# The decay logits of a gated linear attention as one float32r product per half sequence

## Chip, cores and metric

The kernel runs on one core of a Trainium2 chip. The metric is the device time of one execution in microseconds. Before the change it was 1006.1 us (median of 3 runs, 1002.45 to 1006.14).

## What is computed

A decoder trunk of two layers over 1024 tokens of width 1024. Each layer projects the normalised input into three groups of heads (sliding-window attention, retention, gated linear attention), and projects their joined outputs back. The change concerns the decay of the gated linear attention (GLA): 16 low-rank channels `ga` of the input projection are multiplied by a 16x128 matrix, a bias is added, and the logarithm of a sigmoid of it is the decay per token and key channel.

```
proj = h @ w_in
(aq, ak, av, ag, rq, rk, rv, rg, gq, gk, gv, gg, ga) = jnp.split(proj, IN_SPLITS, axis=-1)
...
gate_logits = (ga @ gla_gate_w + gla_gate_b).astype(jnp.float32)
log_a = (jax.nn.log_sigmoid(gate_logits) / GLA_GATE_NORMALIZER).reshape(B, S, GLA_HEADS, GLA_DK)
g = gated_linear_attention(gq, gk, gv, log_a)
```

The tensors are float32. `GLA_GATE_RANK` is 16, and 4 heads of 32 key channels give 128 columns.

## The kernel before

**Tiling.** Tokens lie in 8 tiles of 128 (`t` = 0 to 7). The large products run on TensorE in the type float32r. A float32 operand is kept as two float32r parts, high (the rounded value) and low (the rest), and a product is the sum of three passes: high by high, low by high, high by low (`PASSES`). The arenas hold the parts of the input tiles (`hT`) and of the weights; a weight chunk is loaded into a staging tile `st` by a transfer from SyncE's queue, then split by ScalarE or VectorE (high part) and VectorE or GpSimd (low part).

**Before layer 0.** `mod_first` computes the modulation vectors from `c`; `pre` normalises a token tile: two squares with sums on ScalarE (L654), their sum and scale on VectorE (L643, L637), a power on GpSimd (L638), the scaling on VectorE (L669), eight transposes on TensorE (L178), the modulation (L701 on ScalarE, L703 on VectorE), and the split into high and low (L707, L711). The first two token tiles are prepared while `mod_first` runs, the third and fourth while TensorE works on the first gate products, the other four later.

**Gates.** A layer begins with the gate projections. `do_gates` projects two token tiles for `gg` (272 columns: 256 of the GLA gate and the 16 channels `ga`), then two for `rg` (the retention gate), and so on in layer 0; layer 1 does six tiles of `gg` before `rg`. Each `gg` tile starts `gla_logits` (L993): ScalarE copies the 16 channels out of the PSUM bank (L995), `silu2` computes the gate (L987 on ScalarE, L989 on VectorE) and SyncE stores it to `sgS`. Later the 128x16 copy is transposed by TensorE into 16 rows (L1001), and ScalarE copies these into columns of `gaT` (L1002), whose row 16 and those behind it are ones from a fill (L784).

**Decay logits.** When four token tiles are in `gaT` (32 partitions by 512 tokens), `gla_log` multiplies it by `gwt` (L1011). `gwt` is a 32x128 float32 tile for each layer: 16 rows of the matrix, one row of the bias, and zeros. ScalarE and VectorE turn the result into the log decay (L1014 to L1019). There are two such products per layer, four in all. The tiles 4 to 7 are transposed only after the first product has read `gaT` (`("z", l, 0)`).

**Order.** TensorE runs in the order in which the program is written. That order is decided at build time by a planner: `clk` is a clock of estimated TensorE time, to which `mult` and `transp` add a cost; side work is put in generators (`job`), which go on as soon as `clk` has passed a due time; the table `L` holds these distances. `pump` is called after every 7 products. For a float32 product of 512 columns `mult` adds 4 x 512 / 2400 = 0.853, for a float32r product 512 / 2400 = 0.213. The other engines' orders, and that of SyncE's queue, are made by the framework's scheduler from the program and its dependences.

**Retention.** After the gates the retention runs: `ret_rot` (VectorE, L820 to L825 and L1151) turns the projections, `ret_core` transposes them, ScalarE copies the transposes (L147 by way of `copy("rT", ...)`), TensorE multiplies, VectorE masks (L1173) and updates the state (L1192, L1194). Beside it, VectorE accumulates the modulation rows of the gate and of the next layer from `w_mod` chunks (L365), each after its own transfer into a staging tile, and the weights of the coming stages are loaded and split (L147, L149, L535).

Of the kernel before, what the change touches and what calls it, by code (L numbers as in the profile page):

```python
# [10 lines left out]
F32 = mybir.dt.float32  # L11
F32R = mybir.dt.float32r
I32 = mybir.dt.int32
AF = mybir.ActivationFunctionType
ALU = mybir.AluOpType
AX = mybir.AxisListType

P = 128
# [3 lines left out]
NT = S // P  # L22
# [69 lines left out]
def trunk(ctx: ExitStack, tc: tile.TileContext, ins, cst, out):  # L92
    nc = tc.nc
    V, A, G, T = nc.vector, nc.scalar, nc.gpsimd, nc.tensor
    x_in, c_in, pos_in, w_mod, b_mod, pre_g, post_g, w_in, sinks, gw_in, gb_in, gn_in, w_out = [
        ins[n] for n in _INS
    ]

    cp = ctx.enter_context(tc.tile_pool(name="const", bufs=1))
    bp = ctx.enter_context(tc.tile_pool(name="big", bufs=1))  # L100
    gp = ctx.enter_context(tc.tile_pool(name="work", bufs=2))
# [5 lines left out]
    def nm(s):  # L107
        uid[0] += 1
        return f"{s}_{uid[0]}"
# [4 lines left out]
    def t1(dt=F32):  # L114
        return gp.tile([P, 256], dt, tag="t1", name=nm("t1"), bufs=B1)
# [4 lines left out]
    def small(w, dt=F32):  # L120
        return gp.tile([P, w], dt, tag="sm", name=nm("sm"), bufs=BS)
# [4 lines left out]
    def aux(dt=F32):  # L126
        return ps.tile([P, 512], dt, tag="aux", name=nm("aux"), bufs=8 - MMB)

    def f(ap):
        return ap.bitcast(F32)  # L130
# [20 lines left out]
    def dma(k, dst, src):  # L151
        {"S": nc.sync, "A": A, "P": G}[EN[k]].dma_start(dst, src)
# [24 lines left out]
    def transp(dst, src, idn):  # L177
        T.transpose(dst, src, idn)  # L178
        clk[0] += 0.056 if src.dtype == F32R else 0.109

    def lat(key, l):

        return L[key + "@1"] if l and key + "@1" in L else L[key]
# [4 lines left out]
    def flag(name, lat=0.0):  # L188
        flags[name] = clk[0] + lat
# [41 lines left out]
    def cload(name, dt=F32, eng=nc.sync):  # L231
        a = cst[name]
        t = cp.tile(list(a.shape), dt, name="c_" + name)
        eng.dma_start(t, a)
        return t
# [3 lines left out]
    ident = cload("ident", eng=A)  # L239
# [540 lines left out]
    gat = []  # L780

    def new_ga():
        gat.append(gp.tile([P, NT * P], F32, tag="kT1", name=nm("gaT"), bufs=1)[0:32, 0:512])
        G.memset(gat[-1], 1.0)  # L784
    stR = cp.tile([P, 2, P], F32, name="stR")
    stG = cp.tile([P, 4, 64], F32, name="stG")
    stC = cp.tile([P, 64], F32, name="stC")
# [16 lines left out]
    for l in range(DEPTH):  # L804
        V.tensor_copy(sink8[:, l].rearrange("p (m r) -> p m r", r=2),
                      sinkn[:, 8 * l:8 * l + 8].rearrange("p (r m) -> p m r", r=2))
    gwt = cp.tile([32, 2, P], F32, name="gwt")
    V.memset(gwt, 0.0)
    for l in range(DEPTH):
        nc.sync.dma_start(gwt[0:16, l, :], gw_in[l])  # L810
        nc.sync.dma_start(gwt[16:17, l, :], gb_in[l:l + 1, :])
    def rotary(dst, src, nh, t, kind):

        s4 = src.rearrange("p (h c k) -> p h c k", h=nh, c=2)
        sn = sincos[:, t, 0, kind * 32:kind * 32 + 32]
        cs = sincos[:, t, 1, kind * 32:kind * 32 + 32]
        b = gp.tile([P, 256], F32, tag="tr", name=nm("tr"), bufs=1)
        b4 = b[:, 0:nh * 64].rearrange("p (h c k) -> p h c k", h=nh, c=2)
        d4 = dst.rearrange("p (h c k) -> p h c k", h=nh, c=2)
        V.tensor_tensor(d4, s4, cs.unsqueeze(1).unsqueeze(1).to_broadcast((P, nh, 2, 32)), ALU.mult)  # L820
        snb = sn.unsqueeze(1).to_broadcast((P, nh, 32))
        V.tensor_tensor(b4[:, :, 0, :], s4[:, :, 1, :], snb, ALU.mult)
        V.tensor_tensor(b4[:, :, 1, :], s4[:, :, 0, :], snb, ALU.mult)
        V.tensor_tensor(d4[:, :, 0, :], d4[:, :, 0, :], b4[:, :, 0, :], ALU.subtract)
        V.tensor_tensor(d4[:, :, 1, :], d4[:, :, 1, :], b4[:, :, 1, :], ALU.add)  # L825
# [158 lines left out]
    def silu2(pg):  # L984

        th = t1()
        A.activation(th, pg, AF.Tanh, scale=0.5)  # L987
        sg = t1()
        V.scalar_tensor_tensor(sg, th, 1.0, pg, ALU.add, ALU.mult)  # L989
        return sg  # L990


    def gla_logits(l, t, pg, pa):  # L993
        ga = small(16)
        A.activation(ga, pa, AF.Copy)  # L995
        dma("ssg", sgS[t], silu2(pg))
        yield lat("gz1", l)
        if t >= 4:
            yield (0.0, ("z", l, 0))
        pt = aux()  # L1000
        transp(pt[0:16, 0:P], ga, ident)  # L1001
        A.activation(gat[l][0:16, (t % 4) * P:(t % 4 + 1) * P], pt[0:16, 0:P], AF.Copy)  # L1002
        flag(("ga", l, t), lat("gz2", l))

    las = {}
# [454 lines left out]
    def layer(l):  # L1460
        if l == 0:
            job(table_job())
        new_ga()
        def do_gates(name, p):
            w = used(l, name)
            for t in (2 * p, 2 * p + 1):
                pg = mm()
                if name == "gg":
                    project(pg[:, 0:272], l, t, w, 272)
                    job(gla_logits(l, t, pg[:, 0:256], pg[:, 256:272]))  # L1470
                else:
                    project(pg[:, 0:256], l, t, w)
                    dma("ssr", srS[t], silu2(pg[:, 0:256]))
                pump()
            if p == NP_ - 1:
                load(l, "rk" if name == "gg" else "rv")
            if name == "gg" and p % 2:
                job(gla_log(l, p // 2))
# [228 lines left out]
```

## Time and profile before

| | |
|---|---|
| median of 3 runs | 1006.1 us (1002.45 to 1006.14) |
| span of the profiled execution | 1008.9 us |
| TensorE busy (PE) | 975.4 us, 97% |
| weight loads (PEld) | 829.5 us, 82% |
| VectorE (DVE) | 684.5 us, 68% |
| ScalarE (ACT) | 408.8 us, 41% |
| GpSimd (POOL) | 234.4 us, 23% |

The span is from the first to the last instruction of the profiled execution; the page gives no other time for it.

How to read the lines that follow. A page line of an engine gives its busy time, the share of the span, and the number of instructions. The chain that ended last is followed back from the last instruction, at each step to what released it. A line of the windows gives a stretch in us from the span's start, its length, the busy time and number of instructions of TensorE, weight loads, VectorE, ScalarE and GpSimd, then the granted TensorE clock (1.00 is full speed), the share of the transfer engines and GB/s. A line of the timeline gives the start and the time taken in us, the engine, the line of the kernel, the operation, `output<-inputs` and the shape; "x4" are four instructions that follow each other, and in brackets stand the idle time before the first and what ended it. SPq and ACTq are the transfers issued by SyncE and ScalarE. A line of the grouped instructions ends with the busy time in us, the mean time of one in ns, and the idle time before them. A line of the chain in order of time gives start, time taken and what.

A matmul's record has a latency at its end that overlaps the next one, so the cost of a matmul in a row of them is the distance from start to start.

### The profile page before, as it was taken

Reading aid. Unit: us, or ns where it says so; the run is one execution under the profiler, and the core shown is the slowest. Engines: PE = TensorE matmul, PEld = TensorE weight load, DVE = VectorE, ACT = ScalarE, POOL = GpSimd, SP = SyncE. Lnnn points to the kernel's source line nnn. Section 1 sums busy time; section 2 is a strip of 40 time slices with the busy share of each in tenths; the row PEclk is TensorE's granted clock in tenths of the full one; section 3 lists DMA queues with packets and bytes.
Section 4 is the critical chain, followed back from the end, with each engine's and each line's share of the span. In section 5 each row is a group of like instructions: output and inputs, shape, how many; then the busy total and the mean of one; then the engine's idle time right before and its main releaser. Section 6 shows DMA issues by size and latency. Waiting matters only on the chain.

```text
span 1008.9 us, 19610 instructions
## 1 busy us (share of the span) xinstructions
PE 975.4 (97%) x7137; PEld 829.5 (82%) x7137; DVE 684.5 (68%) x1680; ACT 408.8 (41%) x1152; POOL 234.4 (23%) x275
## 2 busy tenths in 40 slices
PE   5899999899999999999999999999999999999897
PEld 1499999888998777778889999998899877777785
DVE  3789857757666778564578275785666577566876
ACT  2476311223322656632465232123332256663321
POOL 2310001223320234330112000113332034544100
PEclk8899999999999999999999999999999999999999
DMA  9942513623326355577655251353132434378883
GB/s 293 308 137 76 173 45 100 170 81 96 96 74 199 89 149 163 171 239 244 214 157 173 64 158 32 108 150 100 41 104 85 125 90 130 112 236 249 265 263 140
DMA packets 129836, 148.73 MB, mean 147 GB/s; under 512 B 14046, under 2 KB 94152, under 8 KB 129740
## 3 DMA queue, kind: packets, MB, share of 16 engines
q1 hardware_dynamic: 124044, 137.92, 45.3%
q10 hardware_dynamic: 5696, 9.56, 2.6%
q8 instruction: 56, 0.92, 0.4%
q14 instruction: 40, 0.33, 0.1%
HBM read 109.17 MB, written 36.18 MB: 144 GB/s over the span
## 4 chain that ended last, share of the span: by engine, by line
PE 80%; DVE 8%; DMA 7%; issue 2%; POOL 1%; ACT 1%; SPq 0%; POOLq 0%; DVEq 0%; ACTq 0%
PE mm L163 61%; PE aux L163 14%; PE aux L178 5%; DMA st<-in_w_in_dram 2%; DMA st<-in_w_out_dram 1%; POOL sm L638 1%; DMA xk<-in_x_dram 1%; DMA wm<-in_w_mod_dram 1%; DMA t<-aoS 1%; DVE arena L535 1%; DMA st<-in_w_mod_dram 1%; DMA t<-sgS 1%; DVE t L328 0%; DVE st L572 0%; DMA mixF<-t 0%
## 5 line engine op out<-in xcount | busy, mean ns | idle before, releaser
L163 PE MATMUL mm<-arena 128*128 128x256 f32 (+2 forms) x1824 | 299.2, 318 | 1.8 <-ACT arena L707 1.8
L163 PE MATMUL mm<-arena,arena 128*128 128x256 f32 (+2 forms) x1824 | 300.7, 318 | 0.0
L163 PEld LDWEIGHTS mm<-arena 128*128 128x128 f32 x1824 | 254.6, 191 | 26.5 <-issue 4.1
L163 PEld LDWEIGHTS mm<-arena,arena 128*128 128x128 f32 x1824 | 254.1, 189 | 25.5 <-issue 4.6
L638 POOL TENSOR_TENSOR sm<-sm,mhalf 128x1 f32<-128x1 f32 (+1 forms) x64 | 56.1, 877 | 347.0 <-DVE sm L637 328.6
L163 PE MATMUL mm<-arena,mx 128*128 128x512 f32 (+1 forms) x564 | 132.4, 392 | 2.9 <-ACT kept L1335 2.9
L163 PEld LDWEIGHTS mm<-arena,mx 128*128 128x128 f32 x564 | 103.1, 191 | 27.1 <-ACT kept L1335 3.3
L147 ACT ACTIVATE t<-aux 128x256 f32<-128x256 f32 (+2 forms) x124 | 55.7, 467 | 76.1 <-PE aux L178 64.8
L147 ACT ACTIVATE arena<-st 128x512 fp32r<-128x512 f32 x94 | 56.1, 626 | 59.1 <-DMA st<-in_w_in_dram 21.4
L535 POOL TENSOR_TENSOR arena<-st,arena 128x512 fp32r<-128x512 f32 x31 | 43.2, 1395 | 138.9 <-ACT arena L147 100.9
L926 POOL TENSOR_TENSOR smx<-smx,sm 128x512 f32<-128x512 f32 x32 | 36.1, 1127 | 124.3 <-DVE sm L925 116.1
L535 DVE TENSOR_TENSOR arena<-st,arena 128x512 fp32r<-128x512 f32 x77 | 59.5, 795 | 6.1 <-ACT arena L147 4.1
L922 ACT ACTIVATE smx<-smx,sm 128x129 f32<-128x129 f32 x128 | 49.9, 392 | 28.4 <-DVE sm L919 28.4
L178 PE MATMUL aux<-c_ident,t 128*128 128x128 f32 (+1 forms) x292 | 48.8, 285 | 7.6 <-DVE t L669 7.2
L365 DVE SCALAR_TENSOR_TENSOR acc<-st,c_act,acc 128x512 f32<-128x512 f32 x60 | 45.5, 759 | 12.6 <-DMA st<-in_w_mod_dram 12.1
L178 PEld LDWEIGHTS aux<-c_ident,t 128*128 128x128 f32 (+1 forms) x292 | 35.4, 145 | 15.2 <-DVE t L669 9.0
L701 ACT ACTIVATE t<-aux,mod,mod 128x128 f32<-128x128 f32 x68 | 25.9, 458 | 43.8 <-DVE t L1242 18.2
L970 ACT ACTIVATE t<-aux 128x256 f32<-128x256 f32 x32 | 12.3, 383 | 75.5 <-PE aux L163 63.4
L163 PEld LDWEIGHTS aux<-t,mx 32*128 32x128 f32 (+1 forms) x896 | 39.5, 187 | 3.8 <-issue 2.1
L163 PE MATMUL aux<-t,mx 32*128 32x32 f32 (+1 forms) x896 | 40.7, 273 | 0.0
L917 DVE COPY_PREDICATED smx<-c_curmask,aux 128x256 f32<-128x256 int32 x64 | 25.5, 447 | 18.8 <-ACT smx L147 15.3
L1242 DVE SCALAR_TENSOR_TENSOR t<-t,sm,t 128x512 f32<-128x512 f32 x32 | 24.0, 779 | 18.6 <-DMA t<-in_x_dram 11.9
(220 smaller groups left out, 1384.3 us busy)
## 6 DMA issues: line engine op xcount, KB each, us to landing
st<-in_w_in_dram SPq DMA_DIRECT2D x96, 256.0 KB, 3.1
st<-in_w_mod_dram SPq DMA_DIRECT2D x64, 256.0 KB, 3.3
st<-in_w_out_dram SPq DMA_DIRECT2D x52, 256.0 KB, 3.8
mx<-mixS SPq DMA_DIRECT2D x20, 512.0 KB, 6.2
mixS<-t SPq DMA_DIRECT2D x72, 128.0 KB, 2.3
wm<-in_w_mod_dram SPq DMA_DIRECT2D x12, 512.0 KB, 8.0
t<-in_x_dram SPq DMA_DIRECT2D x24, 256.0 KB, 4.8
t<-tabS SPq DMA_DIRECT2D x16, 256.0 KB, 3.7
```

What stands on the lines that cost most here:

```text
L147: A.activation(dst, src, AF.Copy)
L163: T.matmul(dst, lhsT, rhs, start=start, stop=stop)
L178: T.transpose(dst, src, idn)
L365: V.scalar_tensor_tensor(acc, wt, c_act[:, k:k + 1], acc, ALU.mult, ALU.add)
L535: e.tensor_tensor(lo, st, f(hi), ALU.subtract)
L638: G.tensor_tensor(r, r, mhalf[:, :w], ALU.pow)
L701: A.activation(hf[:, ks], at[kt], AF.Identity, scale=gain, bias=shift)
L917: V.copy_predicated(sv, curmask.unsqueeze(1).to_broadcast((P, 2, P)), pv[:, :, n // P - 1, :])
L922: A.activation(sm[:, h, :], sm[:, h, :], AF.Exp, bias=mx[:, h:h + 1], accum_out=sums[:, h:h + 1])
L926: eng("pn").tensor_tensor(sm[:, :, 0:128], sm[:, :, 0:128], rs.unsqueeze(2).to_broadcast((P, 4, P)), ALU.mult)
L970: A.activation(sq, po, AF.Square)
L1242: V.scalar_tensor_tensor(xt[j], yg[j], r, xt[j], ALU.mult, ALU.add)
```

## The change

The product's operands become float32r with 128 contracted rows. `ga` is now a tile of its own (tag `ga`, 6 buffers) with three groups of 16 columns: high, low, high. ScalarE writes the two high groups with one copy (32 columns), and VectorE subtracts the high part from the PSUM value for the low group. The transpose makes 48 rows of it. `gwt` is built from a float32 tile `gwf` (from the `t1` buffers): rows 0 to 15, 16 to 31 and 32 to 47 hold the matrix, rows 48 and 49 the bias, the rest zeros. A copy rounds all of it to float32r, and a subtraction replaces rows 32 to 48 by the low parts. Contracting high, low, high with high, high, low gives the three passes of the split product in one matmul; the rows of ones meet the two bias rows, and zeros from row 50 on.

```diff
     def new_ga():
-        gat.append(gp.tile([P, NT * P], F32, tag="kT1", name=nm("gaT"), bufs=1)[0:32, 0:512])
-        G.memset(gat[-1], 1.0)
+        gat.append(gp.tile([P, NT * P], F32R, tag="kT1", name=nm("gaT"), bufs=1)[:, 0:512])
+        G.memset(f(gat[-1]), 1.0)
...
-    gwt = cp.tile([32, 2, P], F32, name="gwt")
-    V.memset(gwt, 0.0)
+    gwt = cp.tile([P, 2, P], F32R, name="gwt")
+    gwf = t1()
+    V.memset(gwf, 0.0)
     for l in range(DEPTH):
-        nc.sync.dma_start(gwt[0:16, l, :], gw_in[l])
-        nc.sync.dma_start(gwt[16:17, l, :], gb_in[l:l + 1, :])
+        c = slice(P * l, P * l + P)
+        for r in (0, 16, 32):
+            nc.sync.dma_start(gwf[r:r + 16, c], gw_in[l])
+        nc.sync.dma_start(gwf[48:50, c], gb_in[l:l + 1, :].to_broadcast((2, P)))
+    gwv = gwf.rearrange("p (l n) -> p l n", l=2)
+    V.tensor_copy(gwt, gwv)
+    V.tensor_tensor(gwt[32:49], gwv[32:49], f(gwt[32:49]), ALU.subtract)
...
     def gla_logits(l, t, pg, pa):
-        ga = small(16)
-        A.activation(ga, pa, AF.Copy)
+        ga = gp.tile([P, 3, 16], F32R, tag="ga", name=nm("ga"), bufs=6)
+        A.activation(ga[:, 0:3:2], pa.unsqueeze(1).to_broadcast((P, 2, 16)), AF.Copy)
+        V.tensor_tensor(ga[:, 1], pa, f(ga[:, 0]), ALU.subtract)
         dma("ssg", sgS[t], silu2(pg))
         yield lat("gz1", l)
         if t >= 4:
             yield (0.0, ("z", l, 0))
         pt = aux()
-        transp(pt[0:16, 0:P], ga, ident)
-        A.activation(gat[l][0:16, (t % 4) * P:(t % 4 + 1) * P], pt[0:16, 0:P], AF.Copy)
+        transp(pt[0:48, 0:P], f(ga).rearrange("p a n -> p (a n)"), ident)
+        A.activation(gat[l][0:48, (t % 4) * P:(t % 4 + 1) * P], pt[0:48, 0:P], AF.Copy)
```

The product itself (`mult(z, gwt[:, l, :], gat[l], True, True)`) is written as before. The table `L` of the planner is not changed.

## The prediction

> **What bounds the kernel now.** I read the page first: which engine is full, and which work the chain that ended last runs through.
>
> ```profile
> PE 975.4 (97%) x7137; PEld 829.5 (82%) x7137; DVE 684.5 (68%) x1680; ACT 408.8 (41%) x1152; POOL 234.4 (23%) x275
> ...
> PE 80%; DVE 8%; DMA 7%; issue 2%; POOL 1%; ACT 1%; SPq 0%; POOLq 0%; DVEq 0%; ACTq 0%
> ```
>
> TensorE (PE) is busy 97% and carries 80% of that chain. A share is an average, so next come the stretches in which the four changed products lie, with TensorE's busy time in each.
>
> ```profile
> 50.70:196.50 145.80, 145.26 (x1196) 139.83 (x1194) 112.83 (x313) 61.68 (x147) 18.19 (x17) 1.00 0.39 111
> ...
> 431.00:605.00 174.00, 173.96 (x1103) 152.88 (x1103) 108.37 (x249) 72.59 (x200) 27.32 (x32) 1.00 0.58 180
> 605.00:690.00 85.00, 82.32 (x666) 77.35 (x665) 56.66 (x168) 21.18 (x45) 12.85 (x12) 1.00 0.34 102
> ```
>
> In the first two TensorE stands still for 0.54 and 0.04 us. Time taken off it there moves everything behind it forward, as far as the next stall. Those stalls are the third thing I read, with the granted clock (the 1.00, 0.50 after the engines' columns).
>
> ```profile
> 47.10:49.60 2.50, 1.01 (x10) 0.77 (x8) 2.06 (x5) 0.00 (x0) 1.83 (x2) 1.00 0.56 146
> ...
> 199.62 1.23 PE L163 MATMUL aux<-t 64*128 64x128 f32 x8 [3.09 <-ACT t L147]
> ...
> 205.00:206.00 1.00, 1.00 (x8) 1.00 (x7) 0.00 (x0) 0.00 (x0) 0.00 (x0) 0.65 0.01 1
> ...
> 680.77 0.72 PE L163 MATMUL aux<-t 64*128 64x128 f32 x8 [1.28 <-ACT t L147]
> ...
> 946.33 3.92 PE L163 MATMUL mm<-arena,mx 128*128 128x512 f32 x9 [2.89 <-ACT kept L1335]
> ...
> 946.40:948.00 1.60, 1.60 (x4) 1.31 (x5) 1.60 (x4) 0.05 (x1) 0.00 (x0) 0.50 0.67 187
> 948.00:950.00 2.00, 2.00 (x6) 1.54 (x6) 1.38 (x4) 0.68 (x2) 0.26 (x1) 0.55 0.77 206
> ```
>
> A stall has a second price here. After 2.89 and 3.09 us of standing still TensorE got half its clock: in the one case from 946.3 until about 949.8 (a mean of 0.55 over 2 us is 1.8 us at 0.50), so 3.5 us at half rate, 1.7 us lost; in the other from 199.6 until about 205.7, 6.1 us, 3.0 us lost. After the 1.5 us stall ahead of 49.63 the clock stayed at 1.00.
>
> **What is removed: four float32 products.** Each is recorded as two passes.
>
> ```profile
> 577.84 1.12 PE L163 MATMUL aux<-gaT,gwt 32*128 32x512 f32 x2
> 578.89 0.39 PE L178 MATMUL aux<-c_ident,sm 128*16 128x128 f32 x2
> ...
> 687.37 4.81 PE L163 MATMUL mm<-arena 128*128 128x512 f32 x20
> 692.02 0.38 PE L178 MATMUL aux<-c_ident,t 128*128 128x128 f32 x2
> ```
>
> From the start of the product to the start of what follows is 578.89 - 577.84 = 1.05 us. The new product has float32r operands, 128 contracted rows and 512 columns, as the arena products of the second pair: (692.02 - 687.37) / 20 = 0.23 us. One product saves 0.82 us, four 3.3 us. If nothing but one pass were spared, the bound from below would be half of 1.05, or 2.1 us for all four; from above it is 3.3 us. I take 3.3, since the arena rows have the same type and shape.
>
> **What is added on TensorE: nothing that counts.** The 16 transposes still stream 128 identity columns; only the stationary side grows from 16 to 48 columns.
>
> ```profile
> L178 PE MATMUL aux<-c_ident,t 128*128 128x128 f32 x288 | 48.0, 285 | 7.6 <-DVE t L669 7.2 <-DVE mx L1115 0.3
> ...
> L178 PE MATMUL aux<-c_ident,sm 128*16 128x128 f32 x16 | 4.2, 272 | 0.0
> ```
>
> Between 16 and 128 stationary columns lie 13 ns: at most 16 x 13 = 0.2 us, at least nothing. I take nothing.
>
> **What is added on the other engines.** VectorE (DVE) gets 16 subtractions of 128x16 out of PSUM; the nearest row is the 128x16 copy.
>
> ```profile
> 12.81 0.25 DVE L277 COPY sm<-aux 128x16 f32<-128x16 f32 x2
> ...
> 125.00:150.00 25.00, 25.00 (x218) 24.46 (x217) 14.31 (x51) 3.99 (x9) 2.18 (x2) 1.00 0.18 57
> ```
>
> That is 0.13 us each, 2.0 us in all, half of it per layer, plus some 0.8 us for filling, rounding and subtracting the weight tile (256 columns each). In layer 0 TensorE runs without a pause past 125, and in the 25 us after it VectorE is idle for 10.7 us, so a backlog of 2 us is worked off there. If that cover were gone, its price is those 2 us per layer at most. The ScalarE copies into `ga` write 32 columns in place of 16; the 48-row copy out of PSUM is as long per partition as the 16-row one (some ns each). The larger fill of `gaT` has the same 512 columns per partition. All at nothing.
>
> SyncE gets four more small transfers, in front of the gate stores of layer 0.
>
> ```profile
> 52.07 0.43 SPq L810 DMA_DIRECT2D gwt<-in_gla_gate_w_dram  x1
> ...
> 53.29 0.28 SPq L811 DMA_DIRECT2D gwt<-in_gla_gate_b_dram  x1
> 54.94 1.38 SPq L152 DMA_DIRECT2D sgS<-t  x2
> 56.44 0.38 SPq L152 DMA_DIRECT2D st<-in_w_in_dram  x1
> ...
> 59.40 0.88 DVE L669 TENSOR_SCALAR t<-t,sm 128x512 f32<-128x512 f32 x2
> ...
> 106.26 0.41 DVE L820 TENSOR_TENSOR t<-mm,sincos 128x256 f32<-128x256 f32 x1
> ```
>
> Eight at about 0.38 us end near 55.1, where the first store was issued at 54.94: 0.2 us on a store that nothing reads for 100 us. VectorE's rounding of the weights waits for them, but stands in its order behind the scaling of the fifth token tile (59.40 before), after the last should have landed. The weight load issued at 56.44 and those behind it now stand behind two more stores; the first product with these weights is read at 106.26, so even 10 us would be hidden. Nothing.
>
> **What moves.** The orders of TensorE are nearly the same: 0.64 us less on the planner's clock shifts a few transposes by 7 to 10 products. One move on ScalarE (ACT) does count. In the changed program the first copy into `ga` stands between the squares of the third and of the fourth token tile; before, it stood behind all of them, at 53.95.
>
> ```profile
> 43.87 0.61 ACT L654 ACTIVATE t<-mx 128x512 f32<-128x512 f32 x1
> ...
> 45.00 0.19 ACT L654 ACTIVATION_READ_ACCUMULATOR t<-mx 128x1 f32 x1
> 50.33 1.50 ACT L701 ACTIVATE t<-aux,mod,mod 128x128 f32<-128x128 f32 x4 [5.14 <-PE aux L178]
> ...
> 53.95 0.18 ACT L995 ACTIVATE sm<-mm 128x16 f32<-128x16 f32 x1
> ...
> 46.76 0.15 DVE L643 TENSOR_TENSOR sm<-sm 128x1 f32<-128x1 f32 x1
> ...
> 48.09 1.88 DVE L669 TENSOR_SCALAR t<-mx,sm 128x512 f32<-128x512 f32 x2 [0.44 <-POOL sm L638]
> ...
> 45.83 1.41 PE L163 MATMUL mm<-arena 128*128 128x272 f32 x10
> 47.08 1.04 PE L178 MATMUL aux<-c_ident,t 128*128 128x128 f32 x8
> 49.63 1.09 PE L178 MATMUL aux<-c_ident,t 128*128 128x128 f32 x8 [1.52 <-DVE t L669]
> ...
> 52.68 5.92 PE L163 MATMUL mm<-arena,arena 128*128 128x256 f32 x48
> ```
>
> The copy needs the first gate product, whose last matmul is the third of the ten that start at 45.83: it starts at 46.1 and ends near 46.4. ScalarE now waits for that, and the fourth tile's two squares (1.2 us, done at 45.2 before) end near 47.85. Behind them hang VectorE's sum (46.76 before, now 47.9), GpSimd's power, the scaling, and the transposes for which TensorE already stood 1.52 us. Each comes 1.1 us later, so that stall becomes 2.6 us: a loss of 1.1 us. Bounds: 0 if the product ends early enough, and 1.1 plus a clock drop of 1.7 to 3.0 us if 2.6 us is already too long. The rows leave 1.5 to 2.9 us open; 2.6 lies nearer the upper end, but no row shows a drop below 2.89, so I keep the clock in the sum and the drop as a rival.
>
> [...]
>
> The delay should go no further. The second copy into `ga` now stands ahead of the third tile's modulation (50.33 before) and waits for the second gate product, which ends where the 48 arena products begin; modulation, rounding and subtraction (1.5 + 1.2 + 1.3 us) then fit into the 5.9 us of these 48 before TensorE reads that tile, and the fourth follows a projection later.
>
> **Sum.** -3.3 + 1.1 = -2.2 us. The page gives its span of 1008.9 us and no other time for that execution; the other runs took 1002.45 to 1006.14, median 1006.1, so the span is 2.8 above it. Changes of 2 us carry over: 1006.1 - 2.2, rounded to 1004.
>
> **Rivals.**
>
> *The gain is swallowed by the stalls behind it.*
>
> ```profile
> 192.30 5.80 DMA st<-in_w_in_dram
> ```
>
> The stall at 199.62 ends with this weight transfer (the ScalarE copy that TensorE waits for stands behind a conversion that needs it); the 1.28 us at 680.77 are the same wait in layer 1. If such loads land by the clock and not by TensorE's progress, an earlier arrival only waits longer, and 1.1 us of loss at the start is swallowed too, or remains: 1006 to 1007. Against it: those loads wait for buffers that VectorE frees in step with TensorE's products.
>
> *The clock drops in the longer stall at 48 us.* -3.3 + 1.1 + 1.7 to 3.0 = -0.5 to +0.8: 1005.5 to 1007.
>
> *The stall at 199.62 gets shorter than what lowers the clock.* Orders in the retention stretch ahead of it shift by several products, so the ScalarE copy that is late there may come before the weight transfer. Cut from 3.09 to 1.5 us and without 3.0 us of half rate: -2.2 - 4.6 = -6.8, or -8.3 without any stall: 998 to 999.
>
> *Slower: VectorE stands in order behind a mod-weight transfer while TensorE needs it.*
>
> ```profile
> 165.96 5.29 DMA st<-in_w_mod_dram
> ...
> 171.34 0.75 DVE L365 SCALAR_TENSOR_TENSOR acc<-st,c_act,acc 128x512 f32<-128x512 f32 x1 [3.83 <-DMA st<-in_w_mod_dram]
> ...
> 172.48 0.71 PE L163 MATMUL aux<-t 64*128 64x128 f32 x6 [0.54 <-DVE t L963]
> ```
>
> For 3.83 us VectorE waited, and TensorE felt 0.54 of it. In the changed program these accumulations sit elsewhere among the retention work. If TensorE feels nearly the whole transfer (5.3 us), the stall grows by 3.3 to 4.8 us and, from about 2.9 us on, the clock drops for 3.0 more: -2.2 + 6.3 to 7.8 = +4.1 to +5.6, 1010 to 1012. Against it: the planner's distances there are several microseconds, and only one such stall exists now.
>
> *The change does not do what it says*: the type could leave the product at two passes of 1.05 us. Then only the 1.1 us remains, 1007; the arena rows speak against it.
>
> **How the numbers follow.** Forecast 0.40, swallowed 0.13, clock drop 0.12, shorter stall 0.17, VectorE in order 0.15, no faster product 0.03. About 0.5% (5 us) is what a measurement of this kernel can tell from no change. The forecast, swallowed gain, clock drop and unchanged product lie within it. Faster by more: the shorter stall, plus 0.03 for forecast cases that save a part of it: 0.20. Slower by more: VectorE in order, plus 0.05 of the swallowed and clock cases if they fall together: 0.20. Same 0.60. The range runs from the shorter stall, 998.5, to the lower part of the slow case, 1011.
>
> **What would show it.** Right: four single records of the product near 0.4 us each with 0.23 us to the next start; the copy into `ga` at about 46.4 and a stall near 2.6 us ahead of the fourth tile's transposes, with the clock at 1.00 behind it; the stalls near 197, 680 and 945 about 2 us earlier and as long as before. Wrong: two records per product; a clock of 0.5 at 51; a new TensorE stall above 2 us between 105 and 195; a stall near 197 that is gone.

## The result, and the profile after

The changed kernel is slower: a median of 1009.8 us (20 runs, 1006.9 to 1016.23) against 1005.43 us (20 runs, 1000.95 to 1009.52) before on the same chip, a ratio of 1.0047 with a 95% interval of 1.0033 to 1.0062. That is 4.7 us more (3.3 to 6.2), where 2.1 us less were forecast (1004.0 against 1006.1).

The profiled execution of the changed kernel is one of its faster ones (1008.22 us for a span of 1006.5). That of before has a span of 1008.9 us. With the same 1.7 us between span and time it took about 1010.6 us, an estimate, and that is longer than each of the 20 runs. The two spans therefore stand the wrong way round, and only stretches can be compared in them.

First the engines' line of the changed kernel's page.

```profile
PE 970.6 (96%) x7133; PEld 828.4 (82%) x7133; DVE 688.9 (68%) x1698; ACT 411.3 (41%) x1152; POOL 233.5 (23%) x275
```

TensorE does 4 matmuls fewer (7133 for 7137) and is busy 4.8 us less in these two executions; VectorE has 18 instructions more (16 subtractions of the channels, two for the weight tile). The product does what it says, as the timeline of the changed kernel shows (start, time taken, then what; in brackets the idle time before it and what ended it):

```profile
84.94 4.58 PE L163 MATMUL mm<-arena 128*128 128x256 f32 x24 [2.01 <-DVE t L995]
89.84 1.12 PE L163 MATMUL mm<-arena,arena 128*128 128x272 f32 x7 [0.32 <-DVE t L995]
90.80 0.40 PE L163 MATMUL aux<-gaT,gwt 128*128 128x512 f32 x1
91.04 1.91 PE L163 MATMUL mm<-arena,arena 128*128 128x272 f32 x14
...
100.12 3.14 PE L163 MATMUL mm<-arena 128*128 128x256 f32 x24 [0.73 <-DVE t L995]
```

One record of 0.40 us, and 91.04 - 90.80 = 0.24 us to the next start; before it was 1.05. But there are three stalls that the kernel before doesn't have: 2.01, 0.32 and 0.73 us, 3.06 us together, in which a gate product waits for L995. In the changed kernel that is the VectorE multiplication that ends `silu2` (L989 before): it is the last reader of a gate product's PSUM bank, and the `mm` bank is free only behind it. Before, TensorE went through the same place without a pause:

```profile
80.07 6.00 PE L163 MATMUL mm<-arena 128*128 128x256 f32 x48
85.90 1.04 PE L163 MATMUL mm<-arena,arena 128*128 128x272 f32 x7
```

The next view shows why the banks come free late: the instructions of the tanh in `silu2`, what its engine idled for before it, and who waited for it. First the changed kernel, where it is L993.

```profile
L993 ACT ACTIVATE t<-mm x32: 364/384/389, 50.3 to 583.4; 128x256 f32<-128x256 f32 x32
...
its engine sat idle before it (us, times) until:
  DVE ga L1002: 12.5, 11
  PE mm L163: 9.6, 6
who waited for it (us, times):
  DVE t L995: 18.4, 16
```

The same view of the kernel before, where it is L987:

```profile
L987 ACT ACTIVATE t<-mm x32: 356/382/435, 54.0 to 584.5; 128x256 f32<-128x256 f32 x32
...
  PE mm L163: 8.8, 5
...
  DVE t L989: 21.7, 12
```

Before, the tanh waited for TensorE alone. Now ScalarE idled for 12.5 us, 11 times, until L1002, the new subtraction: both read the bank of the same gate product, and the tanh comes second. Follow the bank of the 2.01 us stall through the timeline of the changed kernel, on ScalarE

```profile
77.69 0.20 ACT L1001 ACTIVATE ga<-mm 128x32 fp32r<-128x32 f32 x1
...
83.20 0.63 ACT L707 ACTIVATE arena<-t 128x512 fp32r<-128x512 f32 x1 [3.99 <-DVE t L703]
83.89 0.38 ACT L993 ACTIVATE t<-mm 128x256 f32<-128x256 f32 x1
```

and on VectorE:

```profile
76.92 1.90 DVE L669 TENSOR_SCALAR t<-t,sm 128x512 f32<-128x512 f32 x2 [0.45 <-POOL sm L638]
78.74 0.68 DVE L535 TENSOR_TENSOR arena<-st,arena 128x512 fp32r<-128x512 f32 x1
...
82.14 1.03 DVE L703 TENSOR_SCALAR t<-aux,mod,mod 128x128 f32<-128x128 f32 x3
83.09 0.67 DVE L424 SCALAR_TENSOR_TENSOR t<-t,t 128x512 f32<-128x512 f32 x1
83.69 0.16 DVE L1002 TENSOR_TENSOR ga<-mm,ga 128x16 fp32r<-128x16 f32 x1
83.87 0.69 DVE L711 TENSOR_TENSOR arena<-t,arena 128x512 fp32r<-128x512 f32 x1
84.48 0.41 DVE L995 SCALAR_TENSOR_TENSOR t<-t,mm 128x256 f32<-128x256 f32 x1
```

and the same two engines in the kernel before:

```profile
76.94 0.19 ACT L995 ACTIVATE sm<-mm 128x16 f32<-128x16 f32 x1
77.00 0.40 ACT L987 ACTIVATE t<-mm 128x256 f32<-128x256 f32 x1
```

```profile
81.64 0.41 DVE L989 SCALAR_TENSOR_TENSOR t<-t,mm 128x256 f32<-128x256 f32 x1
```

Before, the tanh ran at 77.00, right behind the copy of the 16 channels, and only the multiplication stood in VectorE's queue. Now the bank goes through that queue twice: the copy is done at 77.9, the subtraction comes up behind modulation and rotation tables (L424) at 83.69, the tanh starts at 83.89, 6 us behind the copy, and the multiplication takes a second place at 84.48. TensorE, which needed the bank at 82.93, goes on at 84.94. ScalarE's own order changed with it: the rounding of the next token tile (L707 at 83.20), which waits 3.99 us for VectorE's modulation, now stands ahead of the tanh, where before it stood behind. At this place it ends at 83.83 and the subtraction at 83.85, so the tanh is late by both.

VectorE was also further behind than before, for another reason: a weight split (L535) and a scaling (L669) of 1.90 us in place of 0.88 us (at 76.49 before) lie in this stretch. GpSimd works on a weight split beside that scaling:

```profile
76.86 1.29 POOL L535 TENSOR_TENSOR arena<-st,arena 128x512 fp32r<-128x512 f32 x1
```

The kernel before shows the same pair at another place: its scaling at 48.09 took 1.88 us, beside a split on GpSimd (48.03, 1.26 us), and the one at 76.49, with no split beside it, 0.88. In split_own (at 79.14) and own_tag (74.44) the scaling takes 1.91 and 1.90 us too, in sub_only and sbuf_split 0.88 and 0.89. The order of the weights' splits came out differently in the changed kernel. The experiments below separate this from the subtraction.

Behind the stall the granted clock falls to 0.50 for a while (from 86.9 to 88.9 us). The windows of the changed kernel around it (the number behind POOL's column is the granted clock):

```profile
83.00:84.90 1.90, 0.00 (x0) 0.00 (x0) 1.89 (x6) 1.65 (x5) 0.00 (x0) 1.00 0.00 0
84.90:88.20 3.30, 3.25 (x19) 3.26 (x20) 3.30 (x10) 2.21 (x7) 0.00 (x0) 0.68 0.12 40
88.20:91.00 2.80, 2.48 (x15) 2.21 (x14) 2.80 (x6) 0.69 (x3) 0.00 (x0) 0.77 0.14 46
91.00:93.00 2.00, 2.00 (x17) 1.95 (x16) 2.00 (x5) 1.71 (x3) 0.00 (x0) 1.00 0.39 132
```

A mean of 0.68 over 3.3 us and of 0.77 over 2.8 us is 3.3 x 0.32 + 2.8 x 0.23 = 1.7 us of clock: the 24 products behind the stall took 4.58 us, for 3.13 at full clock. Here this costs no time, since the next bank is late as well. In after_late, an experiment below, no drop followed a stall of 2.00 us: its 24 products took 3.14 us, the stall behind them is 1.76 us in place of 0.32, and the next products start 4.90 us after the end of the first stall in both kernels (89.84 - 84.94 and 88.84 - 83.94). What the late banks cost is better read from the start of the 48 products to the start of what follows them: 89.84 - 79.80 = 10.04 us, for 85.90 - 80.07 = 5.83 before. That is 4.2 us, and with the 0.73 us at 100.12 it is 4.9 us.

The other place is the stall ahead of the fourth tile's transposes. Timeline of the changed kernel, ScalarE and TensorE:

```profile
44.96 0.20 ACT L1001 ACTIVATE ga<-mm 128x32 fp32r<-128x32 f32 x1 [3.22 <-PE mm L163]
...
49.28 1.09 PE L178 MATMUL aux<-c_ident,t 128*128 128x128 f32 x8 [2.45 <-DVE t L669]
```

The copy stands ahead of the fourth tile's squares, ScalarE idles for 3.22 us until the first gate product is done, and TensorE stands 2.45 us (1.52 before). Here no drop followed: the clock was 1.00 from 49.3 to 52.3.

The two lengths can't simply be subtracted, since TensorE's clock ahead of the stall differs. The 27 matmuls ahead of the third tile's transposes, in the kernel before and then in the changed kernel:

```profile
42.24 5.00 PE L163 MATMUL mm<-arena 128*128 128x272 f32 x27 [1.81 <-ACT arena L707]
```

```profile
40.02 5.93 PE L163 MATMUL mm<-arena 128*128 128x272 f32 x27 [1.81 <-ACT arena L707]
```

They took 5.00 and 5.01 us in the profiles of before and own_tag, and 5.7 to 6.4 us in the ten others. With the copy behind the squares, slower matmuls shorten the stall, since the squares don't wait for them: 1.52 us at 5.00 (before), 0.55 at 5.96 (prod_sm), 0.51 at 6.02 (after_late), 0.34 at 6.18 (sbuf_split). With the copy ahead, the squares wait for the product too: 2.59 us at 5.01 (own_tag), 2.45 at 5.93 (the changed kernel). So the move costs 1.1 us in an execution like the profiled one of before, and about 1.9 us in one like that of the changed kernel. How often the kernel before runs either way, its one profile can't tell.

By the terms at hand: -3.3 (product) + 4.9 (banks) + 1.9 (stall at 48 us) = +3.5 us, or +2.7 with 1.1 for the stall, where 4.7 (3.3 to 6.2) were measured. The gain is eaten by the two waits, and they make the kernel slower.

The granted clock differs too. Each execution lists its span and its mean granted clock; span x (1 - clock) is the part of the clock that was withheld, put as time, and the rest is span x clock. Changed kernel, mean of 20 runs: 15.9 us and 992.7. Kernel before: 11.3 us and 991.7 (23 runs of the third set of experiments), 11.0 and 992.3 (34 of the second). So the changed kernel has about 4.7 us more withheld on average, and the rest grew by 0.4 to 1.0 us (standard errors 0.2 to 0.6 us each). This does not make 4.7 us of clock the cause: the 1.7 us at 85 us cost no time, as shown above, and where the rest lies is not shown, since the two profiled executions hold nearly equal amounts (1008.9 x 0.014 = 14.1 us before and 1006.5 x 0.015 = 15.1 now).

### The profile page after: what moved, and what is told of

It is laid out like the page before. It is cut to its first block, busy times and chain, and to the rows that moved or that the text cites. A ratio compares the mean times of both kernels' runs of the same rounds, so it can differ in the third digit from the quotient of the medians.

```text
span 1006.5 us, 19620 instructions
## 1 busy us (share of the span) xinstructions
PE 970.6 (96%) x7133; PEld 828.4 (82%) x7133; DVE 688.9 (68%) x1698; ACT 411.3 (41%) x1152; POOL 233.5 (23%) x275
## 5 line engine op out<-in xcount | busy, mean ns | idle before, releaser
L163 PE MATMUL mm<-arena 128*128 128x256 f32 (+2 forms) x1824 | 303.2, 320 | 4.6 <-DVE t L995 2.7
L163 PEld LDWEIGHTS mm<-arena 128*128 128x128 f32 x1824 | 258.0, 193 | 29.6 <-DVE t L995 3.3
L535 POOL TENSOR_TENSOR arena<-st,arena 128x512 fp32r<-128x512 f32 x31 | 43.4, 1404 | 135.2 <-ACT arena L147 98.0
L535 DVE TENSOR_TENSOR arena<-st,arena 128x512 fp32r<-128x512 f32 x77 | 59.4, 791 | 6.5 <-ACT arena L147 4.4
```

Of the source, the lines that this page charges most:

```text
L163: T.matmul(dst, lhsT, rhs, start=start, stop=stop)
L535: e.tensor_tensor(lo, st, f(hi), ALU.subtract)
```

## The experiments

Line numbers are the changed kernel's unless something else is said. In `after_late` those of the steps named here are 2 to 3 higher.

### The subtraction behind the gate (late_sub)

```diff
         A.activation(ga[:, 0:3:2], pa.unsqueeze(1).to_broadcast((P, 2, 16)), AF.Copy)
+        sg = silu2(pg)
         V.tensor_tensor(ga[:, 1], pa, f(ga[:, 0]), ALU.subtract)
-        dma("ssg", sgS[t], silu2(pg))
+        dma("ssg", sgS[t], sg)
```

> The same work as the changed kernel; the subtraction for the low part stands behind the gate's tanh and multiplication. Theory W (ScalarE's tanh waits for VectorE's subtraction, since both read one PSUM bank, so the bank is free one pass through VectorE's queue later and TensorE stands 3.1 us for banks and then runs at half clock): without that wait the stalls near 85, 90 and 100 us are gone, and the time falls by 3.1 + about 2 us against the changed kernel, to 0.2% below before (ratio 0.998). Theory D (the 16 added instructions are too much for VectorE): as the changed kernel, 1.004 to 1.005. Theory P (the planner's clock moved TensorE's order): as the changed kernel too, since TensorE's order stays as it is there.

Measured: 1006.91 us (12 runs), ratio 1.0012 (0.9993 to 1.0031), between what was expected by W (0.998) and by D or P (1.004 to 1.005). TensorE's stalls in its timeline:

```profile
84.75 3.11 PE L163 MATMUL mm<-arena 128*128 128x256 f32 x24 [1.45 <-DVE ga L1003]
89.51 1.11 PE L163 MATMUL mm<-arena,arena 128*128 128x272 f32 x7 [1.66 <-DVE ga L1003]
```

The tanh no longer waits for the subtraction, but now the subtraction (L1003 here) is the bank's last reader and sets when it comes free: 1.45 and 1.66 us of bank stalls. No half clock followed the first (24 products in 3.11 us). From the start of the 48 products to what follows them it takes 89.51 - 80.19 = 9.3 us, for 10.04 in the changed kernel and 5.83 before, and the stall near 100 us is gone. So the other order of the two VectorE reads saves 1.4 of the 4.9 us of bank waits (the time fell by 0.35%, 3.5 us, to some 2.4 us), and 3.5 us of them stay: the bank still stands in VectorE's queue a second time.

### The planner's order of before (old_cost)

```diff
-        mult(z, gwt[:, l, :], gat[l], True, True)
+        mult(z, gwt[:, l, :], gat[l], True, True, 4 * 512 / 2400.0)
```

> The changed kernel, with the planner charging the product as before (0.853 in place of 0.213), which restores TensorE's order of before in full. Theory P: the loss is gone, ratio 0.997 to 0.999. Theories W and D: the loss stays, ratio 1.004 to 1.006.

Measured: 1008.59 us (12 runs), ratio 1.0043 (1.0025 to 1.006), and the stalls for banks are there (2.00, 0.28 and 0.70 us). TensorE's order is that of before, so the few transposes that the planner shifts are not the cause, and theory P is out.

### The subtraction without the product (sub_only), the product without the subtraction (prod_only)

In the kernel before:

```diff
-        ga = small(16)
-        A.activation(ga, pa, AF.Copy)
+        ga = gp.tile([P, 3, 16], F32R, tag="ga", name=nm("ga"), bufs=6)
+        A.activation(ga[:, 0:3:2], pa.unsqueeze(1).to_broadcast((P, 2, 16)), AF.Copy)
+        V.tensor_tensor(ga[:, 1], pa, f(ga[:, 0]), ALU.subtract)
...
-        transp(pt[0:16, 0:P], ga, ident)
+        transp(pt[0:16, 0:P], f(ga[:, 0]), ident)
```

> The kernel before with the split alone: the high parts are written twice, the low part is computed by VectorE and not used, and the product stays float32 on the 32 rows with the rounded channels (the low parts are left out of the result). TensorE's order is that of before. Theory W: the whole loss without the product's gain, 0.9 us at 48 us, 3.1 us of bank stalls and about 2 us of half clock: +6, ratio 1.006, up to 1.008 if the product had saved 3.3 in the changed kernel. Theory P: ratio 1.001 (the 0.9 us alone).

In the changed kernel:

```diff
-        ga = gp.tile([P, 3, 16], F32R, tag="ga", name=nm("ga"), bufs=6)
-        A.activation(ga[:, 0:3:2], pa.unsqueeze(1).to_broadcast((P, 2, 16)), AF.Copy)
-        V.tensor_tensor(ga[:, 1], pa, f(ga[:, 0]), ALU.subtract)
+        ga = gp.tile([P, 1, 16], F32R, tag="ga", name=nm("ga"), bufs=6)
+        A.activation(ga[:, 0], pa, AF.Copy)
...
-        transp(pt[0:48, 0:P], f(ga).rearrange("p a n -> p (a n)"), ident)
+        transp(pt[0:16, 0:P], f(ga[:, 0]), ident)
```

> The float32r product alone: the high parts of channels, matrix and bias, one ScalarE copy and no subtraction (the low parts are left out of the result). Theory W: the product's 3.3 us less, the stall at 48 us 0.9 us longer: -2.4, ratio 0.9976. Theory P: this kernel has TensorE's order of the changed kernel, so ratio 1.003 or more.

prod_only also leaves out the weight tile's low parts: the subtraction for them and four of its eight loads.

Measured: sub_only 1014.23 us (6 runs), ratio 1.0083 (1.0055 to 1.0111); prod_only 1003.94 us (12 runs), ratio 0.9993 (0.9969 to 1.0016). The subtraction and the own buffers for `ga` alone cost 8.3 us; with the faster product this is 4.7, so the product is worth about 0.0036 x 1005 = 3.6 us there, to some 3 us. Without the subtraction TensorE's timeline lists no stall for a bank, and 1.0047 - 0.9993 = 0.0054, or 5.4 us (to some 2.8 us), is gone with it. In prod_only the stall near 48 us stays, and behind it the clock is halved (its timeline, then its windows):

```profile
50.83 1.97 PE L178 MATMUL aux<-c_ident,t 128*128 128x128 f32 x8 [2.23 <-DVE t L669]
```

```profile
50.80:52.00 1.20, 1.17 (x6) 1.18 (x7) 1.20 (x3) 0.00 (x0) 0.72 (x1) 0.50 0.43 95
52.00:54.00 2.00, 2.00 (x11) 2.00 (x10) 0.10 (x1) 0.00 (x0) 1.08 (x1) 0.50 0.11 6
```

### The copy's buffers alone (own_tag), and the product with the old buffers (prod_sm)

In the kernel before, `ga = small(16)` becomes `gp.tile([P, 16], F32, tag="ga", name=nm("ga"), bufs=6)`; in prod_only, the own tile becomes `small(16, F32R)`.

> The kernel before, with nothing but the buffers of the channels' copy changed: six of their own in place of the shared small ones. The first copy then stands on ScalarE ahead of the fourth tile's squares, as in the changed kernel. Theory S (that move makes the stall at 48 us longer): that stall is 2.5 us in place of 1.5, ratio 1.001. If the move costs nothing: 1.000 and 1.5 us.

> As prod_only (high parts alone, the low parts are left out), with the copy in the shared small buffers, so that it stands behind the squares again. Theory S: 1 us less than prod_only, the product's 3.3 us in full, ratio 0.9965 to 0.998, stall at 48 us 1.5 us. Otherwise 0.999 as prod_only.

Measured: own_tag 1007.6 us (12 runs), ratio 1.0027 (1.0011 to 1.0044); prod_sm 1003.12 us (12 runs), ratio 0.998 (0.9966 to 0.9994). With buffers of its own the first copy goes ahead of the fourth tile's squares in the scheduler's order, without any subtraction. The stall is 2.59 us in own_tag and 0.55 in prod_sm. The move alone costs 2.7 us (1.1 to 4.4) in the one comparison and 0.0013 x 1005 = 1.3 us, to some 2.8 us, in the other (prod_only against prod_sm). In own_tag half clock followed the stall (0.50 from 52 to 54), as in prod_only.

### The subtraction from a copy in SBUF (sbuf_split), on GpSimd (sbuf_pool)

```diff
+        raw = small(16)
+        A.activation(raw, pa, AF.Copy)
+        sg = silu2(pg)
         ga = gp.tile([P, 3, 16], F32R, tag="ga", name=nm("ga"), bufs=6)
-        A.activation(ga[:, 0:3:2], pa.unsqueeze(1).to_broadcast((P, 2, 16)), AF.Copy)
-        V.tensor_tensor(ga[:, 1], pa, f(ga[:, 0]), ALU.subtract)
-        dma("ssg", sgS[t], silu2(pg))
+        A.activation(ga[:, 0:3:2], raw.unsqueeze(1).to_broadcast((P, 2, 16)), AF.Copy)
+        V.tensor_tensor(ga[:, 1], raw, f(ga[:, 0]), ALU.subtract)
+        dma("ssg", sgS[t], sg)
```

sbuf_pool has `G.tensor_tensor` in place of `V.tensor_tensor`.

> The changed kernel, but ScalarE copies the 16 channels once out of the PSUM bank into a buffer of the shared small ones, as before, and high and low parts are made from that copy; VectorE still does all 16 subtractions. Late_sub still showed waits of 1.45 and 1.66 us for banks, now behind the subtraction itself. Theory B (not the wait of the tanh alone, but any second pass through VectorE's queue before the bank is free): no wait for banks near 85, 90 and 100 us, and the stall at 48 us back at 1.5 us, since the first copy stands behind the squares again; the product's 3.3 to 3.6 us remain whole, ratio 0.9965 to 0.998. Theory D (16 more instructions on VectorE): 1.001 or more, as late_sub.

> As sbuf_split, with the 16 subtractions on GpSimd, so VectorE has none. Theory B: as sbuf_split, 0.9965 to 0.998. Theory D: clearly below sbuf_split.

Measured: sbuf_split 1001.67 us (12 runs, 998.17 to 1005.77), ratio 0.9969 (0.9949 to 0.9988), the only version with all three passes that is clearly faster than the kernel before (prod_sm leaves the low parts out): 3.1 us (1.2 to 5.1) less. sbuf_pool 1003.27 us (12 runs), ratio 0.9988 (0.9972 to 1.0003), a little above what was expected and not clear of sbuf_split. Timeline of sbuf_split, TensorE, and what the tanh (L993) waited for:

```profile
47.25 1.09 PE L178 MATMUL aux<-c_ident,t 128*128 128x128 f32 x8 [0.34 <-DVE t L669]
...
77.59 5.99 PE L163 MATMUL mm<-arena 128*128 128x256 f32 x48
83.42 1.04 PE L163 MATMUL mm<-arena,arena 128*128 128x272 f32 x7
84.31 0.40 PE L163 MATMUL aux<-gaT,gwt 128*128 128x512 f32 x1
```

```profile
L993 ACT ACTIVATE t<-mm x32: 365/382/428, 51.6 to 578.1; 128x256 f32<-128x256 f32 x32
...
  PE mm L163: 9.4, 6
```

VectorE does the same 16 subtractions, ScalarE even 16 copies more, and no bank is late: the 48 products run through again, and the tanh waits for TensorE alone. So it is not VectorE's load that costs; what is left is where the subtraction reads, where the first copy stands, and the order of the weight splits that came with these edits. That GpSimd in its place brings nothing fits this.

### The two causes apart (after_late, split_own)

sbuf_split changes two things, since its copy is back in the shared buffers. after_late keeps the changed kernel and only queues the copy behind the fourth tile's squares; split_own is sbuf_split with the raw copy in buffers of its own.

```diff
-            A.activation(to[j], xt[j], AF.Square, accum_out=ss[:, j:j + 1])
+            sq.append(A.activation(to[j], xt[j], AF.Square, accum_out=ss[:, j:j + 1]))
...
-        A.activation(ga[:, 0:3:2], pa.unsqueeze(1).to_broadcast((P, 2, 16)), AF.Copy)
+        with tc.issue_after(sq[7].ins):
+            A.activation(ga[:, 0:3:2], pa.unsqueeze(1).to_broadcast((P, 2, 16)), AF.Copy)
```

> The changed kernel with one instruction moved back: the first copy into ga on ScalarE is queued behind both squares of the fourth token tile, as before the change; the orders of the other engines stay as in the changed kernel. Theory (the bank wait is the larger loss, the prologue the smaller): the stall ahead of the fourth tile's transposes near 49 us falls from 2.45 to 0.3 to 1.5 us, the bank stalls near 85, 90 and 100 us remain (3 us together); time 0.1 to 0.25% under the changed kernel's 1.0047, so 1.002 to 1.0035 of the kernel before. Rival (the prologue is the main loss and brings the bank stalls with it): the bank stalls go too, and the time falls to 0.997.

```diff
-        raw = small(16)
+        raw = gp.tile([P, 16], F32, tag="raw", name=nm("raw"), bufs=3)
...
-        ga = gp.tile([P, 3, 16], F32R, tag="ga", name=nm("ga"), bufs=6)
+        ga = gp.tile([P, 3, 16], F32R, tag="ga", name=nm("ga"), bufs=5)
```

> The version whose subtraction reads a copy in SBUF, but with that copy in buffers of its own (3, and 5 instead of 6 for ga), so that the first copy again stands ahead of the fourth tile's squares, as in the changed kernel. Theory: the stall near 49 us is 2.2 to 2.6 us again, no stall for a bank behind VectorE appears between 80 and 105 us, and the time lies 0.1 to 0.25% above the SBUF version's 0.9969: 0.998 to 0.9995 of the kernel before. Rival (the earlier place of the copies is what makes the bank wait costly): bank stalls of over 1 us return, and the time is 1.002 or more.

Measured: after_late 1006.02 us (12 runs), split_own 1005.75 us (12 runs). With the two others they make a square:

| ratio to before | copy ahead of the squares | copy behind them |
|---|---|---|
| subtraction reads PSUM | 1.0047 (1.0033 to 1.0062) | after_late 1.0011 (0.9993 to 1.003) |
| subtraction reads SBUF | split_own 1.0008 (0.9989 to 1.0026) | sbuf_split 0.9969 (0.9949 to 0.9988) |

Along each row the copy's place is worth 0.36 and 0.39%, down each column the place that is read 0.39 and 0.42%: about 3.8 and 4.1 us (each difference to some 2.5 us, by its two intervals). sbuf_split comes from another set of runs and another chip than after_late and split_own; each ratio is to the kernel before, run beside it. Both expectations were off by size: the copy's place came out above the 0.1 to 0.25% written there, though the intervals reach into that, and within what can be told it costs as much as the bank wait. TensorE's stalls in the timeline of after_late:

```profile
48.29 1.09 PE L178 MATMUL aux<-c_ident,t 128*128 128x128 f32 x8 [0.51 <-DVE t L671]
...
83.94 3.14 PE L163 MATMUL mm<-arena 128*128 128x256 f32 x24 [2.00 <-DVE t L997]
88.84 1.13 PE L163 MATMUL mm<-arena,arena 128*128 128x272 f32 x7 [1.76 <-DVE t L997]
```

and of split_own, with its windows behind the first stall:

```profile
50.04 1.82 PE L178 MATMUL aux<-c_ident,t 128*128 128x128 f32 x8 [2.02 <-DVE t L669]
...
85.87 3.11 PE L163 MATMUL mm<-arena 128*128 128x256 f32 x24 [0.79 <-ACT t L993]
```

```profile
50.00:52.00 2.00, 1.96 (x10) 1.96 (x11) 1.40 (x4) 0.00 (x0) 1.51 (x1) 0.56 0.33 71
52.00:54.00 2.00, 2.00 (x12) 2.00 (x11) 0.00 (x0) 0.00 (x0) 0.30 (x1) 0.58 0.11 14
```

after_late has the bank stalls (2.00, 1.76, and 0.72 us at 99) and a short stall at 48. Its 4.5 us of bank stalls are no more waiting than the changed kernel's 3.06: there the half clock fills a part of it. split_own has the long stall at 48, with 2 x 0.44 + 2 x 0.42 = 1.7 us of clock behind it, and 0.79 us for a bank (the view names a tanh that ends at the same time as the bank's multiplication, 85.73). Nothing behind the stall at 48 hides its half clock: from the resumption to the start of the 48 gate products it takes 31.9 us in split_own (50.04 to 81.96), and 30.5 us in the changed kernel (49.28 to 79.80) and in after_late (48.29 to 78.80), so the drop costs 1.4 us there. The left column and the upper row of the square are clean: after_late and split_own keep the weight splits of the changed kernel around 80 us. In sbuf_split those splits lie elsewhere, so the other two differences hold that as well.

For the bank of the first stall, from the timelines (us; the last but one column is counted from the start of the 48 gate products, which need the bank after 3.13):

| | copy | tanh | multiplication | bank free | stall |
|---|---|---|---|---|---|
| before | 76.94 | 77.00 | 81.64 | 1.98 | none |
| sbuf_split | 74.47 | 74.53 | 79.86 | 2.68 | none |
| own_tag | 80.02 | 80.08 | 84.76 | 3.01 | none |
| sub_only | 78.19 | 83.18 | 83.77 | 3.57 | 0.52 |
| split_own | 79.37 | 79.43 | 85.32 | 3.77 | 0.79 |
| changed | 77.69 | 83.89 | 84.48 | 5.09 | 2.01 |

Where the subtraction reads PSUM ahead of the tanh, the tanh comes 5 to 6 us behind the copy, otherwise 0.06 us. sub_only has the subtraction without the weight splits: 0.52 us, and 1.76 at the next bank. split_own has the weight splits without the read of PSUM: 0.79. The changed kernel has both. From the start of the 48 products to what follows them it takes 5.83 us before and in sbuf_split, 6.86 in split_own, 8.52 in sub_only and 10.04 in the changed kernel. Of the 4.9 us that the banks cost there, some 1.0 is thus the weight splits' and some 3.9 the subtraction's (the stall near 100 us included, which split_own doesn't have). Which line of the change moved the weight splits wasn't tried.

## Why the prediction was wrong

**The product.** Right: one record of 0.40 us, 0.24 us to the next start, -3.3 us. The runs give 3.6 (sub_only against the changed kernel), 2.0 (prod_sm) and 3.1 us (sbuf_split, where all that the product needs is kept), each to some 1.5 to 3 us.

**What is added on TensorE, and SyncE's transfers.** Nothing in the runs speaks against the nothing that was taken: with all of it, sbuf_split is 3.1 us (1.2 to 5.1) faster.

**What is added on the other engines.** This is the step that failed. It counted the 16 subtractions as 2.0 us of VectorE's time behind which TensorE keeps running, "all at nothing". It did not count that the subtraction, a new reader of the gate product's PSUM bank, is a wait: the tanh stands behind it, the multiplication behind the tanh, and TensorE needs that bank three products later. Its duration is 0.16 us; its place in the queues is some 3.9 of the 4.9 us that the late banks cost. And the step looked at VectorE from 125 us on, where there is slack; the banks are short from 80 to 100, and from 80 to 90 VectorE was busy 10.00 of 10 us before. There the changed order of the weight splits, which the prediction did not look at, made it later still. By the square, reading PSUM costs 3.9 us (left column) and 4.2 us (right).

**What moves.** The mechanism was right in each part: the copy ahead of the squares (at 44.96, the gates having begun 2.2 us earlier and run slower in this execution), the stall of 2.45 us for the forecast 2.6. The price was taken too low: 1.1 us, with "1.1 plus a clock drop of 1.7 to 3.0 us" as the other end. That the length came out is no proof of the price: the 1.52 us that was subtracted belongs to an execution with quick first matmuls (5.00 us). There 1.1 us is right, as own_tag shows (2.59 us), but in an execution like that of the changed kernel the stall without the move is about 0.5 us, and the move costs 1.9. Half clock can come on top, 1.4 us in split_own. The comparisons of times give 1.3 (prod_only against prod_sm), 2.7 (own_tag), 3.6 (after_late) and 3.9 us (split_own against sbuf_split), 2.9 on average.

**The sum** with the sizes of the square: -3.3 + 3.9 + 3.6 = +4.2 us; measured were 4.7 (3.3 to 6.2). The 3.9 and 3.6 contain the measured 1.0047 themselves, so this is bookkeeping and no test; the sum from the traces, +2.7 to +3.5 us, uses no measured time of a kernel, and falls short of the 4.7 by 1 to 2 us, which the runs do not place.

**The rivals.** *The clock drop in the longer stall at 48 us* did not come in the profiled execution of the changed kernel, but it did in those of prod_only, split_own and own_tag, behind 2.23, 2.02 and 2.59 us. In four others with the copy ahead (the changed kernel, old_cost, late_sub, sub_only; 2.45 to 2.60 us) it didn't. The rival's sum, -0.5 to +0.8, lacked the bank wait. *Slower, VectorE in order*: the right engine and the right form, a bank that TensorE needs behind VectorE's queue, but at the wrong place and behind table work instead of a mod-weight transfer. *The gain swallowed by stalls behind it*: no; sbuf_split keeps 3.1 us through the same stalls. *The shorter stall at 199.62*: in part; it was 2.29 us in the changed kernel for 3.09, and half clock still followed, but less of it (a mean of 0.79 from 199 to 207, for 0.58 before). *The product unchanged*: no.

**The marks.** The product, the 48 us stall and its clock in that execution (1.00 from 49.3 to 52.3) came as written, and so did the copy's place. The mark for wrong, a stall above 2 us between 105 and 195, began too late: the stall lay at 83 to 85 us. The stalls near 680 and 945 did not keep their length (2.02 for 1.28, 1.69 for 2.89), and a stall of 1.50 us for a transfer came at 956, which the profile of before doesn't have.

## What to carry to other kernels

Cost a new instruction that reads PSUM by its place in its engine's queue, not by its duration: here 0.16 us of subtraction held the bank, and the tanh that reads it next, until VectorE's queue got to it, 5 to 6 us behind the copy. Let one engine drain the bank and take everything else from its copy; that was 7.8 us here (1.0047 against 0.9969), together with the second point: giving a tile buffers of its own can move its first writer forward in an engine's order, in front of work on the critical path (own_tag: the stall at 48 us was 2.59 us for 1.52). Half clock behind a stall counted here only where nothing later waited anyway: it cost 1.4 us behind the stall at 48 us in split_own, and nothing at 85 us, where the next bank was late. And take a stall's length from more than one execution before subtracting it: the 1.52 us of before was 0.3 to 0.6 us in the four other profiles with the copy behind the squares.

## What was not expected of the hardware

ScalarE's read of a PSUM bank started only behind VectorE's read of other columns of the same bank: it idled for this 12.5 us, 11 times, and in sbuf_split not once. Whether the chip needs this or only the program's semaphores ask for it, these runs cannot tell.

The granted clock stood at 0.50 behind stalls of 2.01 us (the changed kernel, from 86.9 to 88.9), 2.02 (split_own, from 51 to 53), 2.23 (prod_only, from 50.8 to 54) and 2.59 us (own_tag, from 52 to 54). By TensorE's pace it also fell behind 2.00 us (old_cost, at 84.1: 24 products in 4.62 us, for 3.13) and 1.76 (sub_only, at 89.1: the float32 product in 2.04 us, for 1.12). It did not fall behind 2.60 (old_cost, at 48.4: the next 17 products in 2.37 us, for 3.75 in own_tag), 2.58 (late_sub and sub_only, near 50: 2.39 us), 2.45 (the changed kernel, at 49.3: a clock of 1.00), 2.00 (after_late, at 83.9: 1.00, 24 products in 3.14 us) or 1.76 (after_late, at 88.8: 1.00). So between 1.8 and 2.6 us the length alone does not decide, and what does, no run here shows. The prediction had taken 2.89 as the shortest that does; but in the kernel before, too, the clock stood at 0.50 from 42.2 to 45.2 us, behind a stall of 1.81.
